# A quarter turn of an 8192 x 8192 matrix: whole loads and two early stores in halves, in place of five loads in three pieces

## The chip, the cores and the metric

The kernel runs on one core of a Trainium2 chip. The metric is the device time of one launch in microseconds. The kernel before took 1281.91 us, the median of three runs that lie between 1279.8 and 1283.59 us. The profiled execution has a span of 1280.1 us from its first to its last instruction, and all times inside a profile are counted from the start of that span.

## The reference

```python
def setup_inputs():
    return {
        "x": np.random.randn(8192, 8192).astype(np.float32),
        "k": 1,
    }

def reference(x: np.ndarray, k: int) -> np.ndarray:
    return np.rot90(x, k)
```

With k = 1 the output element in row i and column j is x[j, 8191 - i]. Nothing is computed; 268.44 MB are read from device memory and 268.44 MB are written back in another order.

## The kernel before

The input is cut into macro tiles of 1024 rows by 4096 columns (eight row tiles of 128 rows each), sixteen of them; the last one is cut again in two halves of four row tiles. A macro tile goes through four steps:

1. **Load.** A row tile of 128 rows x 4096 columns (2 MB, 16 KB in each partition) is loaded into SBUF by a DMA that the SP queue issues. It takes one of two buffers of `a_pool`; in the first macro tile some go to `o_pool`, which stands empty then.
2. **Reverse.** VectorE copies it in eight chunks of 512 columns into buffers of `r_pool` (63 of them, of 2 KB a partition), and turns the order of the columns within each block of 128.
3. **Transpose.** TensorE transposes 128 x 128 blocks into PSUM, 32 for each output.
4. **Store.** ScalarE copies two PSUM tiles of 128 x 2048 into an output tile (16 KB in each partition, three buffers in `o_pool`) and issues the DMA that stores it, from its own queue. A macro tile has eight outputs. Each needs all eight row tiles of its macro tile, one 512-column chunk from each.

The loop that loads. `loads` counts the row tiles, so every 25th is loaded in three pieces, of which the two outer ones have 8 rows:

```python
P = 128
R = 1024
RT = R // P
W = 4096
CH = 512
EVERY = 25
UNEVEN = [(0, 8), (8, P - 8), (P - 8, P)]
F = 4096
FP = 2048
# ... cut ...
    a_pool = ctx.enter_context(tc.tile_pool(name="a_pool", bufs=2))
    r_pool = ctx.enter_context(tc.tile_pool(name="r_pool", bufs=63))
    o_pool = ctx.enter_context(tc.tile_pool(name="o_pool", bufs=3))
    psum_pool = ctx.enter_context(
        tc.tile_pool(name="psum", bufs=2, space=bass.MemoryType.PSUM)
    )
# ... cut ...
        for t in range(rt):
            if loads < RT and loads % 5 >= 2:
                a = o_pool.tile([P, W], dt, tag="o")
            else:
                a = a_pool.tile([P, W], dt, tag="a")
            loads += 1
            for p0, p1 in UNEVEN if loads % EVERY == 0 else [(0, P)]:
                r = r0 + t * P
                nc.sync.dma_start(
                    out=a[p0:p1, :], in_=x[r + p0 : r + p1, c0 : c0 + W]
                )
            for j in range(W // CH):
                ar = r_pool.tile([P, CH // P, P], dt, tag="ar")
                nc.vector.tensor_copy(
                    out=ar[:],
                    in_=a[:, j * CH : (j + 1) * CH].rearrange(
                        "r (b m) -> r b m", m=P
                    )[:, :, ::-1],
                )
                chunks[t, j] = ar
```

The loop that stores. For a macro tile of 1024 rows PW is 2 and G is 4: an output tile holds four groups of 1024 numbers in each partition. S is how many groups go out with one DMA; in the kernel before it is 4 everywhere but in the very last output of the kernel:

```python
        for i, g0 in enumerate(range(0, W // P, G)):
            # ... cut: the output tile ot, from o_pool (every other one from
            # a_pool in the two last, smaller tiles) ...
            o = ot[:, : G * rows].rearrange("m (g f) -> m g f", g=G)
            S = PW if end and r0 + rows == N and g0 + G == W // P else G
            # ... cut: the first output's transposes run tile by tile ...
            for h in range(0, G, PW):
                if h // PW not in ps:
                    psum_tile(h // PW)
                    for w in range(h, h + PW):
                        for t in range(rt):
                            transposes(t, [w])
                nc.scalar.copy(o[:, G - PW - h : G - h, :], ps[h // PW])

                done = h + PW
                if done % S == 0:
                    top = M - c0 - (g0 + done) * P
                    dst = out[top : top + S * P, r0 : r0 + rows].rearrange(
                        "(g m) f -> m g f", g=S
                    )
                    nc.scalar.dma_start(
                        out=dst, in_=o[:, G - done : G - done + S, :]
                    )
```

A pass over the finished program (`whole_reads`) merges the SBUF side of every store into one contiguous read per partition: 16 KB where S is 4, 8 KB where S is 2.

Of the kernel before, what the change touches and what calls it, by code (L numbers as in the profile page):

```python
# [2 lines left out]

# [5 lines left out]
# [8 lines that stand above are left out]
LAST = [4, 4]  # L17
W = 4096
CH = 512
EVERY = 25  # L20
UNEVEN = [(0, 8), (8, P - 8), (P - 8, P)]
F = 4096
FP = 2048


def whole_reads(nc):

    for fn in nc.m.functions:
        for block in fn.blocks:
            for n, ins in enumerate(block.instructions):
                if not isinstance(ins, mybir.InstDMACopy):
                    continue
                src = ins.ins[0]
                ap = [list(d) for d in src.ap]
                if len(ap) == 3 and ap[2][0] == 1 and ap[1][0] == ap[2][1]:  # L40
                    ap = [ap[0], [1, 1], [1, ap[1][1] * ap[2][1]]]
                    block.instructions[n] = copy.replace(
                        ins,
                        ins=[copy.replace(src, ap=ap)],
                        ant_dge_precooked=False,
                    )


def macro_tiles(N, M):

    tiles = [(r0, RT, c0) for r0 in range(0, N, R) for c0 in range(0, M, W)]
    r0, _, c0 = tiles.pop()
    for n in LAST:
        tiles.append((r0, n, c0))
        r0 += n * P
    return tiles


@with_exitstack
def kernel(  # L60
    ctx: ExitStack,
    tc: tile.TileContext,
    x: bass.AP,
    k: bass.AP,
    out: bass.AP,
):
    nc = tc.nc
    assert k == 1, f"only k=1 supported, got {k}"
    nc.at_finalize(whole_reads)

    N, M = x.shape
    dt = x.dtype

    consts = ctx.enter_context(tc.tile_pool(name="consts", bufs=1))
    ident = consts.tile([P, P], dt)
    make_identity(nc, ident)
# [8 lines that stand above are left out]
    loads = 0  # L85

    def load(r0, rt, c0):

        nonlocal loads
        chunks = {}
# [5 lines that stand above are left out]
            else:  # L100
                a = a_pool.tile([P, W], dt, tag="a")
            loads += 1

            for p0, p1 in UNEVEN if loads % EVERY == 0 else [(0, P)]:
                r = r0 + t * P
                nc.sync.dma_start(  # L108
                    out=a[p0:p1, :], in_=x[r + p0 : r + p1, c0 : c0 + W]
                )  # L110
            for j in range(W // CH):
                ar = r_pool.tile([P, CH // P, P], dt, tag="ar")
                nc.vector.tensor_copy(  # L113
# [6 lines that stand above are left out]
            yield chunks  # L120

    def store(r0, rt, c0, chunks, end):

        rows = rt * P
        PW = 1
        while 2 * PW * rows <= FP:  # L130
            PW *= 2
        G = PW
        while 2 * G * rows <= F:
            G *= 2
        for i, g0 in enumerate(range(0, W // P, G)):
            if end and i % 2:
                ot = a_pool.tile([P, F], dt, tag="a")
            else:
                ot = o_pool.tile([P, F], dt, tag="o")
            o = ot[:, : G * rows].rearrange("m (g f) -> m g f", g=G)  # L140

            S = PW if end and r0 + rows == N and g0 + G == W // P else G


            ps = {}

            def transposes(t, ws):
                for w in ws:
                    g = g0 + w
                    nc.tensor.transpose(  # L150
                        ps[w // PW][:, PW - 1 - w % PW, t * P : (t + 1) * P],
                        chunks[t, g * P // CH][:, g % (CH // P), :],
                        ident,
                    )

            def psum_tile(h):
                pt = psum_pool.tile([P, FP], mybir.dt.float32, tag="ps")
                ps[h] = pt[:, : PW * rows].rearrange("m (g f) -> m g f", g=PW)

            if i == 0 and (rt == RT or r0 + rows < N):  # L160
                for h in range(G // PW):
                    psum_tile(h)
                for t in range(rt):
                    transposes(t, range(G))
# [17 lines that stand above are left out]
            yield  # L182

    tiles = macro_tiles(N, M)
    *most, before_last, last = tiles
    for m in most:
        *_, chunks = load(*m)
        for _ in store(*m, chunks, False):
            pass


    *_, chunks = load(*before_last)
    outputs = store(*before_last, chunks, True)
    rows = load(*last)
    for _ in range(last[1] - 1):
        next(rows)
    next(outputs)
    chunks = next(rows)
    for _ in outputs:
        pass  # L200
    for _ in store(*last, chunks, True):
        pass


# [1 line left out]
_INS = ['x', 'k']  # L206
_OUTS = [((8192, 8192), 'float32')]

_NUMBERS = {'k': 1}


# [26 lines left out]
```

## Time and profile before

| what | value |
|---|---|
| device time, median of three | 1281.91 us |
| span of the profiled execution | 1280.1 us |
| bytes moved by DMA, mean rate over the span | 537.55 MB, 420 GB/s |
| row tile loads: whole / in three pieces | 123 / 5 |
| output stores: whole / in two halves | 127 / 1 |
| busy: TensorE, VectorE, ScalarE | 54%, 28%, 37% of the span |
| median time from issue to landing: whole load, whole store | 16.6 us, 25.5 us |

The profile's page cuts the span in 40 slices of 32 us. For each slice it gives the busy tenths of each engine, the mean busy share of the sixteen DMA engines, and the bytes moved in GB/s. A table by windows gives the same for any stretch that is asked for: its length, the busy time of each engine with the number of its instructions, the granted TensorE clock, the busy share of the DMA engines (successive packets overlap by a little in the records, so 1.01 stands for full) and the rate in GB/s. The timeline of an engine lists its instructions in order; in brackets at the end of a line stands how long the engine was idle before it, and what ended that wait.

### The profile page before, as it was taken

The numbers are of one execution on the slowest core, as the hardware profiler recorded it, in microseconds if no ns is written. First come the engines' busy times: TensorE is split into PE (matmuls) and PEld (weight loads), VectorE is DVE, ScalarE is ACT, GpSimd is POOL, SyncE is SP. The second block draws the span as 40 slices with busy tenths as digits, with TensorE's granted clock in tenths as the row PEclk, the third lists the DMA queues.
The fourth block names the chain that finished last, engine by engine and source line by source line (L and its number), as shares of the span: only waits on it lengthen the run. The fifth ranks groups of instructions, "written<-read, shape, count | busy, mean of one in ns | idle before, by whom it ended". The sixth has DMA issues, their size and how long they took to land.

```text
span 1280.1 us, 10428 instructions
## 1 busy us (share of the span) xinstructions
PE 688.8 (54%) x4096; PEld 640.3 (50%) x4096; DVE 355.2 (28%) x1024; ACT 468.1 (37%) x257; POOL 0.7 (0%) x6
## 2 busy tenths in 40 slices
PE   1565556545465555655546545565554645536673
PEld 1455555545464444554536535554454644535673
DVE  4423222232223222223222232223222232223220
ACT  0433334334243432433424424243432443325353
POOL 0000000000000000000000000000000000000000
PEclk9976777868778676776777758677677786777677
DMA  9999999999999999999999999999999999999998
GB/s 401 426 429 429 429 428 398 429 430 428 429 428 429 405 420 429 413 430 428 428 428 399 428 373 428 429 429 428 430 414 429 412 431 427 427 428 418 409 424 341
DMA packets 37137, 537.55 MB, mean 420 GB/s; under 512 B 4192, under 2 KB 4192, under 8 KB 4192
## 3 DMA queue, kind: packets, MB, share of 16 engines
q1 hardware_dynamic: 18512, 268.44, 50.0%
q10 hardware_dynamic: 18576, 268.44, 49.7%
q8 instruction: 32, 0.52, 0.2%
q14 instruction: 17, 0.14, 0.0%
HBM read 268.44 MB, written 268.44 MB: 419 GB/s over the span
## 4 chain that ended last, share of the span: by engine, by line
DMA 81%; DVE 12%; ACT 3%; PE 2%; issue 1%; ACTq 0%; DVEq 0%; SPq 0%
DMA a<-in_x_dram 76%; DVE ar L113 12%; DMA out_dram<-ot 4%; ACT ot L171 3%; PE pt L150 2%; ACTq L179 0%; DVEq L113 0%; SPq L108 0%; ACTq L171 0%
## 5 line engine op out<-in xcount | busy, mean ns | idle before, releaser
L150 PE MATMUL pt<-ident,ar 128*128 128x128 f32 x4096 | 688.8, 345 | 572.2 <-ACT ot L171 377.3
L150 PEld LDWEIGHTS pt<-ident,ar 128*128 128x128 f32 x4096 | 640.3, 183 | 620.5 <-ACT ot L171 414.2
L171 ACT COPY ot<-pt 128x2048 f32<-128x2048 f32 x256 | 466.8, 1870 | 769.6 <-DMA out_dram<-ot 466.3
L113 DVE COPY ar<-a 128x512 f32<-128x512 f32 x1024 | 355.2, 420 | 883.8 <-DMA a<-in_x_dram 757.8
L171 ACT ACT_TABLE_LOAD x1 | 1.3, 1283 | 25.6 <-DVE ar L113 25.6
masks.py:199 POOL TENSOR_SCALAR_AFFINE_SELECT ident<-ident 128x128 f32<-128x128 f32 x1 | 0.3, 292 | 0.1
masks.py:197 POOL MEMSET ident<- 128x128 f32 x1 | 0.2, 205 | 0.3 <-POOLq L219 0.3
L219 POOL MEMSET const-bfloat16-1.0<- 128x1 bf16 x1 | 0.1, 102 | 0.0
L219 POOL MEMSET const-uint8-127<- 128x1 uint8 x1 | 0.1, 102 | 0.0
L219 POOL MEMSET const-float32-0.0<- 128x1 f32 x1 | 0.1, 99 | 0.2 <-issue 0.2
L219 POOL MEMSET const-float32-1.0<- 128x1 f32 x1 | 0.1, 99 | 0.0
## 6 DMA issues: line engine op xcount, KB each, us to landing
out_dram<-ot ACTq DMA_DIRECT2D x127, 2048.0 KB, 25.5
a<-in_x_dram SPq DMA_DIRECT2D x123, 2048.0 KB, 16.6
a<-in_x_dram SPq DMA_DIRECT2D x5, 1792.0 KB, 18.7
out_dram<-ot ACTq DMA_DIRECT2D x2, 1024.0 KB, 15.0
a<-in_x_dram SPq DMA_DIRECT2D x10, 128.0 KB
```

What stands on the lines that cost most here:

```text
L113: nc.vector.tensor_copy(out=ar[:], in_=a[:, j * CH : (j + 1) * CH].rearrange("r (b m) -> r b m", m=P)[:, :, ::-1],)
L150: nc.tensor.transpose(ps[w // PW][:, PW - 1 - w % PW, t * P : (t + 1) * P], chunks[t, g * P // CH][:, g % (CH // P), :], ident,)
L171: nc.scalar.copy(o[:, G - PW - h : G - h, :], ps[h // PW])
L219: nc = _bacc.Bacc("TRN2", target_bir_lowering=False, num_devices=1)
```

## The change: what it does and what it is for

It has two parts. First, the five row tiles whose number is a multiple of 25 are loaded as all others are, with one DMA of 128 rows; the pieces of 8, 112 and 8 rows are gone. Second, the fifth and the seventh output of the first macro tile (i is 4 and 6) are stored in two halves: S is 2 for them, so each half is one DMA of 1 MB whose SBUF reads are 8 KB, and the first half is issued after the first of the two ScalarE copies. While these halves are in the queue beside whole loads, a read of the store queue is half as large as one of the load queue; the second part is there to change how the two queues share the DMA engines for that time. What is computed stays the same.

```diff
-EVERY = 25
-UNEVEN = [(0, 8), (8, P - 8), (P - 8, P)]
 F = 4096
 FP = 2048
# ... cut ...
             loads += 1
-            for p0, p1 in UNEVEN if loads % EVERY == 0 else [(0, P)]:
-                r = r0 + t * P
-                nc.sync.dma_start(
-                    out=a[p0:p1, :], in_=x[r + p0 : r + p1, c0 : c0 + W]
-                )
+            nc.sync.dma_start(
+                out=a[:], in_=x[r0 + t * P : r0 + (t + 1) * P, c0 : c0 + W]
+            )
# ... cut ...
-            S = PW if end and r0 + rows == N and g0 + G == W // P else G
+            lead = r0 == 0 and c0 == 0 and i in (4, 6)
+            S = PW if lead or (end and r0 + rows == N and g0 + G == W // P) else G
```

The order of the instructions on every engine stays as it was, but for the ten DMA issues that fall away on the SP queue and the two that are added on ScalarE's.

## The prediction

> **What bounds the kernel now.** I first read the page. TensorE is busy for 54% of the span, VectorE for 28%, ScalarE for 37%, so none of them is full. The DMA row and the row of rates under it tell the rest:
>
> ```profile
> DMA  9999999999999999999999999999999999999998
> GB/s 401 426 429 429 429 428 398 429 430 428 429 428 429 405 420 429 413 430 428 428 428 399 428 373 428 429 429 428 430 414 429 412 431 427 427 428 418 409 424 341
> ...
> q1 hardware_dynamic: 18512, 268.44, 50.0%
> q10 hardware_dynamic: 18576, 268.44, 49.7%
> ```
>
> The reader is to see that the sixteen DMA engines are taken all the time, and that most slices stand at 428 to 430 GB/s, while some ten fall to between 373 and 420. Nothing is left to win in a slice at 429. What the kernel could lose or gain lies in the dips, and since the engines never have a reserve, a dip is not made up later. Loads (q1) and stores (q10) take half of the engines each.
>
> Second, I asked the chain that ended last where the dips are. It is mostly load after load: a VectorE copy of eight chunks, then about 16.6 us until the next load of that buffer has landed. Five of its loads are longer: 21.0 us from 196.75, 19.7 from 437.27, 20.8 from 697.44, 19.4 from 945.39 and 20.1 from 1185.85. At about 9.8 us a row tile (two loads in each 19.5 us of the chain) these are the places of the row tiles 25, 50, 75, 100 and 125, the ones in three pieces. The chain leaves the loads twice, at 759 and at 914 us, for outputs.
>
> Third, I cut the span around these places with the table by windows (columns: stretch, its us, then the compute engines, the clock, the DMA share and GB/s):
>
> ```profile
> 100.00:190.00 90.00, 51.49 (x284) 48.52 (x284) 24.96 (x72) 32.83 (x18) 0.00 (x0) 0.71 1.01 429
> 190.00:210.00 20.00, 9.98 (x68) 9.07 (x68) 4.93 (x15) 7.74 (x5) 0.00 (x0) 0.75 1.01 379
> ...
> 430.00:465.00 35.00, 20.61 (x132) 19.22 (x132) 8.32 (x24) 14.65 (x8) 0.00 (x0) 0.73 1.01 400
> ...
> 515.00:525.00 10.00, 6.79 (x34) 6.39 (x35) 2.77 (x8) 5.50 (x3) 0.00 (x0) 0.54 0.99 389
> ...
> 670.00:712.00 42.00, 25.39 (x154) 24.00 (x155) 11.09 (x32) 18.29 (x10) 0.00 (x0) 0.70 1.00 405
> ...
> 752.00:769.00 17.00, 8.71 (x50) 8.31 (x51) 5.55 (x16) 6.82 (x4) 0.00 (x0) 0.57 0.86 322
> ...
> 935.00:960.00 25.00, 13.88 (x79) 13.40 (x80) 6.13 (x18) 10.91 (x6) 0.00 (x0) 0.70 1.01 410
> ...
> 1185.00:1212.00 27.00, 18.48 (x93) 17.77 (x91) 5.65 (x17) 8.03 (x5) 0.00 (x0) 0.66 1.01 403
> ```
>
> Two kinds of dip are to be seen. Around the loads in pieces (190, 430, 670, 935, 1185) the engines stay full, a share of 1.00 or 1.01, and yet move less: the same packets take longer. At 515 and 752 the share itself falls, to 0.99 and 0.86; there was not enough to transfer. These lie where a macro tile begins.
>
> Fourth, ScalarE's timeline at the first output of a macro tile, where it waits for TensorE, which waits for the last of eight loads:
>
> ```profile
> 116.95 3.64 ACT L171 COPY ot<-pt 128x2048 f32<-128x2048 f32 x2 [13.08 <-PE pt L150]
> ...
> 277.61 3.64 ACT L171 COPY ot<-pt 128x2048 f32<-128x2048 f32 x2 [15.70 <-PE pt L150]
> ...
> 434.97 3.64 ACT L171 COPY ot<-pt 128x2048 f32<-128x2048 f32 x2 [15.06 <-PE pt L150]
> 517.41 3.64 ACT L171 COPY ot<-pt 128x2048 f32<-128x2048 f32 x2 [18.05 <-PE pt L150]
> ...
> 759.49 3.64 ACT L171 COPY ot<-pt 128x2048 f32<-128x2048 f32 x2 [21.75 <-PE pt L150]
> ...
> 996.34 3.63 ACT L171 COPY ot<-pt 128x2048 f32<-128x2048 f32 x2 [18.25 <-PE pt L150]
> ```
>
> The number in brackets is how long ScalarE had nothing to copy. During it the store queue lives on what was issued before. The wait is 13.1 and 12.3 us at the first two boundaries, 15.7 after row tile 25, 18.0 after 50, 21.8 after 75; after the break at 759 it is 14.7 twice, and 18.3 after 100. So it grows by some 3 us with each load in pieces, and where it reaches 18 us the store queue runs dry: the windows at 515 and 752 are just these two boundaries.
>
> [...]
>
> **The change part by part.**
>
> *Loads in pieces, removed.* Loss of a window = (429 - rate) / 429 x length: 190 to 210 us 2.33, 430 to 465 us 2.37, 670 to 712 us 2.35, 935 to 960 us 1.11, 1185 to 1212 us 1.64; the sum is 9.8 us, all on the path, since the DMA engines are the path. The ten SP issues that fall away, of some 0.33 us each, lie beside other work: 0.
>
> *Boundaries.* In the same way: 515 to 525 us 0.93, 752 to 769 us 4.24, and two more windows of the same answer, 990 to 1010 us at 404 GB/s 1.17 and 1150 to 1170 us at 410 GB/s 0.89; sum 7.2 us. If the wait stays near 13 us, as at the first two boundaries, all of it goes.
>
> *Balance.* [...] In the last 5 us of the span only an engine or two still move data, so one engine's lag sets the end. [...] -3 to +3 us, counted as 0.
>
> *Store halves, added.* Two more issues on ScalarE at 0.55 us, beside its wait of 6.1 us before each copy: 0. [...] the loads get 4.9 us more for each, if buffers let them: some 10 us for both. No bytes are added, so this saves nothing by itself; it moves loads ahead of stores, and the wait at the boundaries from 13 to perhaps 3 to 8 us, so that none runs dry.
>
> *Sum.* 1281.9 - 9.8 - 7.2 = 1264.9, rounded to 1265.
>
> **The rivals.** (1) *The pieces were what kept the sixteen engines together.* Then without them the lag grows, boundaries run dry in spite of the halves, and the time is 1272 if only the direct loss goes, or above 1282 if more is lost. For it: a lag at the end is there. Against it: the boundary wait hardly moves where no piece falls (13.1 to 12.3, 14.7 to 14.7) and jumps where one does. (2) *The halves do nothing or harm:* the reads of 8 KB count as half as fast, or the loads that run ahead stand before VectorE, which waits for a free chunk of the 63, and give the gain back. Then the time is that of removal alone, 1265 to 1270. For it: VectorE already waits for TensorE at times, 126 us in all. (3) *The ends are all that counts:* the slow windows are hidden. That would leave 1281, but full engines with no reserve speak against it.
>
> **Range and chances.** The 9.8 us I hold for nearly sure; of the 7.2 some may come back elsewhere, and the end may go either way by 3. That gives 1260 to 1272. Faster by over 2% means below 1256.3, more than everything counted here and the best case at the end together; 3%. Slower by over 2% needs rival 1 in full: 2%.
>
> **What would show it.** In the profile after: q1 with 18,432 packets and q10 with 18,864; no slice below some 420 GB/s but the first and last; no load of 19 to 21 us in the chain; ScalarE's wait at the boundaries below 13 us throughout, falling right after the first macro tile. A wait that grows without the pieces, or a share below 1 at a boundary, would prove rival 1. A first boundary still at 13 us would prove rival 2 in its first form.

## The result and the profile after

The changed kernel takes 1267.49 us, the median of six runs between 1266.92 and 1267.88; the kernel before takes 1282.1 us in the same comparison. The ratio is 0.9888 with a 95% interval of 0.9876 to 0.9901: 14.6 us are gone. The profiled execution has a span of 1265.4 us in place of 1280.1.

From the page of the changed kernel, the rates in 40 slices and the two DMA queues (q10 stores, q1 loads):

```profile
GB/s 398 428 428 430 427 428 429 429 431 428 428 429 427 430 429 430 428 430 429 428 428 430 429 430 428 428 430 428 429 430 428 429 427 430 426 428 427 428 380 355
...
q10 hardware_dynamic: 18864, 268.44, 50.0%
q1 hardware_dynamic: 18432, 268.44, 49.7%
```

Every slice between the first and the last two stands at 426 to 431 GB/s; the dips to 373 to 420 are gone. One new dip has come, 380 GB/s, just before the end. The packets are as many as the prediction named: 18,432 for 128 loads and 18,864 for 131 stores, 144 for each DMA whether it moves 2 MB or 1 MB. In the kernel before a load in three pieces took 160, (18,512 - 123 x 144) / 5.

The table by windows, at six of the places where the kernel before fell to 322 to 410 GB/s (stretch, its us, compute engines, clock, DMA share, GB/s), and the new dip from a second table of the same kernel:

```profile
190.00:210.00 20.00, 13.37 (x68) 12.89 (x68) 5.55 (x16) 7.27 (x4) 0.00 (x0) 0.66 1.00 428
430.00:465.00 35.00, 22.58 (x120) 21.87 (x121) 8.32 (x24) 13.14 (x8) 0.00 (x0) 0.67 1.01 429
515.00:525.00 10.00, 5.94 (x32) 5.70 (x32) 2.77 (x8) 3.63 (x2) 0.00 (x0) 0.66 1.02 433
670.00:712.00 42.00, 26.16 (x144) 25.03 (x142) 11.26 (x33) 14.54 (x8) 0.00 (x0) 0.71 1.00 428
752.00:769.00 17.00, 9.74 (x53) 9.51 (x54) 5.39 (x16) 7.27 (x4) 0.00 (x0) 0.71 1.01 429
935.00:960.00 25.00, 15.65 (x82) 14.94 (x80) 7.89 (x23) 8.20 (x5) 0.00 (x0) 0.69 1.01 429
```

```profile
1205.00:1232.00 27.00, 20.32 (x139) 19.10 (x140) 4.01 (x12) 17.64 (x10) 0.00 (x0) 0.81 0.89 373
```

ScalarE's timeline at the first output of the third and the twelfth macro tile:

```profile
191.92 3.63 ACT L167 COPY ot<-pt 128x2048 f32<-128x2048 f32 x2 [6.13 <-PE pt L146]
...
900.27 3.64 ACT L167 COPY ot<-pt 128x2048 f32<-128x2048 f32 x2 [6.13 <-PE pt L146]
```

The wait of 12 to 22 us for the last load of a macro tile has vanished. After the first macro tile these are the only two boundaries where a wait of more than 4 us is put down to TensorE, and 6.1 us is what ScalarE waits before any copy, for an output buffer to be stored. The chain of waits has changed with it: it ran through loads for 76% of the span before, now it runs through stores for 81%.

In what follows the loss of a window is, as in the prediction, (429 - rate) / 429 times its length.

### The profile page after: what moved, and what is told of

Read it like the earlier page. It is cut to its first block, busy times and chain, and to the rows that moved or that the text cites. A ratio compares the mean times of both kernels' runs of the same rounds, so it can differ in the third digit from the quotient of the medians.

```text
span 1265.4 us, 10391 instructions
## 1 busy us (share of the span) xinstructions
PE 721.2 (57%) x4096; PEld 680.0 (54%) x4096; DVE 355.2 (28%) x1024; ACT 466.6 (37%) x257; POOL 0.7 (0%) x6
## 3 DMA queue, kind: packets, MB, share of 16 engines
q10 hardware_dynamic: 18864, 268.44, 50.0%
q1 hardware_dynamic: 18432, 268.44, 49.7%
## 4 chain that ended last, share of the span: by engine, by line
DMA 84%; ACT 13%; issue 1%; PE 0%; ACTq 0%; DVE 0%; SPq 0%
DMA out_dram<-ot 81%; ACT ot L167 13%; DMA a<-in_x_dram 3%; PE pt L146 0%; ACTq L175 0%; DVE ar L106 0%; ACTq L167 0%; SPq L101 0%
## 5 line engine op out<-in xcount | busy, mean ns | idle before, releaser
L146 PE MATMUL pt<-ident,ar 128*128 128x128 f32 x4096 | 721.2, 357 | 526.2 <-ACT ot L167 470.2
L146 PEld LDWEIGHTS pt<-ident,ar 128*128 128x128 f32 x4096 | 680.0, 191 | 567.2 <-ACT ot L167 505.0
```

Of the source, the lines that this page charges most:

```text
L146: nc.tensor.transpose(ps[w // PW][:, PW - 1 - w % PW, t * P : (t + 1) * P], chunks[t, g * P // CH][:, g % (CH // P), :], ident,)
```

## The experiments

### Each part by itself

Whole loads, no halved stores:

```diff
-            lead = r0 == 0 and c0 == 0 and i in (4, 6)
-            S = PW if lead or (end and r0 + rows == N and g0 + G == W // P) else G
+            S = PW if end and r0 + rows == N and g0 + G == W // P else G
```

> The loads are whole, no store is halved. Theory A (the pieces cost 9.8 us in their own windows and, through a growing wait at the boundaries, 7.2 us more; the halves only move loads ahead and cost some 3 us at the end, where the store queue of the changed kernel ran dry at 1210 to 1228 us): the wait of ScalarE at the first boundary is 13 us again and stays between 12 and 17 us, no window at a boundary falls below 420 GB/s but perhaps a late one, the gap near the end is gone or smaller, and the time is 1264 to 1267 us. Rival B (the halves are what keeps the boundaries full): the wait grows beyond 18 us without them, boundaries run dry as before, and the time is 1270 to 1275 us.

It takes 1268.03 us (four runs, 1267.17 to 1268.48; ratio to the kernel before 0.9893, 0.9878 to 0.9908). Of the 14.6 us the whole loads bring 13.9. ScalarE's wait at two of its boundaries:

```profile
116.79 3.64 ACT L166 COPY ot<-pt 128x2048 f32<-128x2048 f32 x2 [13.13 <-PE pt L145]
...
983.48 3.63 ACT L166 COPY ot<-pt 128x2048 f32<-128x2048 f32 x2 [14.45 <-PE pt L145]
```

It is between 12.2 and 14.7 us at all fourteen, where the kernel before went from 12 to 22: without the pieces the wait hardly grows (12.7 us at 904, 14.5 at 983), as theory A says. But five late boundaries still dip, where theory A allowed for a late one: 746 to 764 us at 414 GB/s, 905 to 921 at 416, 980 to 1001 at 406, 1063 to 1080 at 408, 1143 to 1158 at 423; 3.3 us in all. The engines are not idle in these windows, their share is 1.00 to 1.01. From 985 to 994 us, in the deepest of them, the queues have (packets, MB, share of the engines' time)

```profile
q1 hardware_dynamic: 153, 2.21, 68.4%
q10 hardware_dynamic: 83, 1.16, 30.4%
```

The stores have less to move, and the loads have 68.4% of the time; but they move 2.21 MB in it, where 68.4% of 429 GB/s over 9 us would be 2.64. The stores move what their share gives, 1.16 MB where 30.4% would be 1.17. Why load rows are slow there was not tested. In return there is no gap near the end: from the windows of this kernel,

```profile
980.00:1001.00 21.00, 13.45 (x89) 12.53 (x90) 5.55 (x16) 10.92 (x6) 0.00 (x0) 0.74 1.00 406
...
1205.00:1232.00 27.00, 20.61 (x154) 19.17 (x153) 5.55 (x16) 15.66 (x10) 0.00 (x0) 0.89 1.00 423
```

The same 27 us stand at 373 GB/s in the changed kernel, a loss of 3.5 us. So the two halves took away 3.3 us at the boundaries and cost about as much at the end.

The five loads in pieces, the two outputs halved:

```diff
-            S = PW if end and r0 + rows == N and g0 + G == W // P else G
+            lead = r0 == 0 and c0 == 0 and i in (4, 6)
+            S = PW if lead or (end and r0 + rows == N and g0 + G == W // P) else G
```

> The five loads stay in pieces, the two outputs are halved. Theory A: the dips around the pieces stay at about 2 us each (9.8 us in all), but the boundaries no longer run dry in the first half of the run, since the wait starts some 10 us lower and grows by 3 us for each load in pieces. The time is 1281.9 - 7.2 + 3 for the gap at the end, some 1275 to 1279 us. Rival B (the halves make the gain): 1268 to 1271 us. Rival C (the halves do nothing without whole loads): 1281 to 1283 us.

It takes 1282.17 us (ratio 1.0002, 0.9992 to 1.0013): nothing is gained, as rival C has it, though not for its reason. The halves do work: the wait at the third boundary is 9.5 us in place of 15.7. But each load in pieces then adds 3.4 to 4.6 us (9.0 to 13.6, 12.3 to 16.9, 16.0 to 19.3), and the later boundaries dip all the same. Windows at three of these boundaries and at one load in pieces:

```profile
747.00:771.00 24.00, 14.78 (x100) 13.62 (x100) 5.55 (x16) 11.01 (x6) 0.00 (x0) 0.72 0.95 380
...
909.00:930.00 21.00, 15.22 (x100) 14.06 (x100) 5.55 (x16) 11.01 (x6) 0.00 (x0) 0.72 0.99 396
933.00:961.00 28.00, 17.71 (x86) 17.24 (x87) 7.72 (x23) 10.91 (x6) 0.00 (x0) 0.65 1.01 405
990.00:1014.00 24.00, 14.40 (x100) 13.16 (x100) 5.55 (x16) 11.01 (x6) 0.00 (x0) 0.73 0.94 371
```

With 832 to 850 us (402 GB/s) and 1154 to 1171 (404) the boundaries lose 9.7 us, more than the 7.2 that the prediction counts for the kernel before; the five windows around the pieces lose 6.7.

One half only, the fifth output, with whole loads:

```diff
-            lead = r0 == 0 and c0 == 0 and i in (4, 6)
+            lead = r0 == 0 and c0 == 0 and i == 4
```

> Whole loads, and only the fifth output is halved: half the lead. Theory A: the first boundary waits some 8 us, no boundary runs dry, and the gap near the end shrinks from 3 us to 0 to 1.5 us; 1264 to 1266 us, the fastest of all. Rival (the gap near the end does not come from the lead): 1267 us as the changed kernel.

It takes 1267.0 us (1266.73 to 1267.79; ratio 0.9887, 0.9872 to 0.9901), the same as the changed kernel. The expectation missed twice: no boundary waits 8 us for TensorE, and the gap stays (1202 to 1228 us at 380 GB/s, 3.0 us). The second half adds no lead that lasts. In the first 150 us loads and stores move 42.24 and 21.04 MB with one half, 42.22 and 20.99 with two, 41.45 and 21.81 with none. The second half does push the loads ahead at first, 5.29 MB against 3.33 from 110 to 130 us of the changed kernel. Then VectorE waits for a free chunk, which TensorE still has to read:

```profile
135.38 2.77 DVE L106 COPY ar<-a 128x512 f32<-128x512 f32 x8 [6.82 <-PE pt L146]
```

The next load waits up to 10.1 us for VectorE, and from 130 to 140 us the lead of the second half is given back:

```profile
q10 hardware_dynamic: 212, 3.06, 72.4%
q1 hardware_dynamic: 92, 1.25, 29.1%
```

### What is slow about a load in pieces

The first three runs keep the two halved outputs and change how the row tiles 25, 50, 75, 100 and 125 are cut. First 112 and 16 rows:

```diff
-UNEVEN = [(0, 8), (8, P - 8), (P - 8, P)]
+UNEVEN = [(0, P - 16), (P - 16, P)]
```

> As the kernel with pieces and halves, but the pieces are of 112 and 16 rows[...]. Theory A1 [...]: dips of 1.5 to 2.5 us around each of the five loads stay, and the time is as with 8, 112 and 8 rows, 1275 to 1279 us. Rival A2 [...]: the dips are gone, 1267 to 1269 us.

It takes 1274.0 us (ratio 0.9939, 0.9922 to 0.9955), between what A1 and A2 forecast. The windows come from the slowest of its four runs, 1277.15 us; the others take 1273.38 to 1274.58. The dips stay: 1.40, 1.12, 1.64, 1.19 and 1.54 us, 6.9 together, as much as the 6.7 of 8, 112 and 8 rows. The third of them:

```profile
678.00:705.00 27.00, 16.43 (x96) 15.67 (x95) 6.96 (x21) 8.85 (x5) 0.00 (x0) 0.75 1.00 403
```

A2 forecast no dips, and falls as to these. How the rows of a piece are shared out among the engines no view shows. In all, the kernel is 8 us faster than with 8, 112 and 8 rows. Its wait starts lower and stays lower (13.5 us at the last boundaries in place of 16.8 to 19.3), and the worst of its boundaries, 980 to 1010 us at 399 GB/s, loses 2.1 us.

Then two pieces of 64 rows:

```diff
-UNEVEN = [(0, 8), (8, P - 8), (P - 8, P)]
+UNEVEN = [(0, 64), (64, P)]
```

> As the kernel with pieces and halves, but the five loads are cut into two pieces of 64 rows[...]. Theory A1 ([...] being cut in two costs nothing): no dip above 0.5 us at the five places, the wait at the boundaries does not grow by more than 1 us at each, 1267 to 1269 us. Rival A3 (any cut of a load costs[...]): dips of 1 to 1.5 us each and a growing wait stay, 1272 to 1275 us as with 112 and 16 rows.

It takes 1277.91 us (ratio 0.9981, 0.9972 to 0.999). Theory A1, by which two pieces of 64 rows should cost nothing, falls: they cost more than 8, 112 and 8 rows, not less. Rival A3 has the direction, but less than the size. The window around the second of these loads, and the next, undisturbed one:

```profile
430.00:456.00 26.00, 13.46 (x79) 12.99 (x80) 6.79 (x20) 10.56 (x6) 0.00 (x0) 0.80 1.01 397
456.00:678.00 222.00, 124.34 (x724) 117.02 (x721) 61.90 (x179) 80.65 (x45) 0.00 (x0) 0.78 1.01 429
```

The five lose 2.33, 1.94, 2.18, 1.82 and 2.18 us, 10.4 together. The stores beside them, which are whole, are slow too: from 430 to 456 us they have 50.2% of the engines' time and move 5.19 MB, or 200 GB/s, while in the 222 us after it 50.6% of the time gives 215 GB/s.

Last, the same five loads in two halves by columns, with one store halved near each so that neither queue gains on the other:

```diff
+TRAIL = [25, 50, 75, 100, 125]
+BOTH = [16, 41, 66, 91, 116]
 # ... cut ...
+            for w in [0, W // 2] if loads in TRAIL else [None]:
+                c, n = (0, W) if w is None else (w, W // 2)
+                nc.sync.dma_start(
+                    out=a[:, c : c + n],
+                    in_=x[r0 + t * P : r0 + (t + 1) * P, c0 + c : c0 + c + n],
+                )
 # ... cut ...
-            lead = r0 == 0 and c0 == 0 and i in (4, 6)
+            stores += 1
+            lead = (r0 == 0 and c0 == 0 and i in (4, 6)) or stores in BOTH
```

> The changed kernel, with the same five loads cut into two halves by columns instead of by rows (all 128 partitions, 8 KB packets), and one output beside each of them halved too, so that neither queue gains on the other. As many DMAs, pieces and bytes as with two pieces of 64 rows[...]. Theory A4 [...]: no dip above 0.5 us at the five places, 1267 to 1269 us. Rival A3 (the cut itself costs): dips of 2 us each, 1276 to 1279 us as with two pieces of 64 rows.

It takes 1267.82 us (1267.66 to 1267.98; ratio 0.9888, 0.9872 to 0.9905). The windows around the second and the third of the loads:

```profile
425.00:450.00 25.00, 17.06 (x107) 16.07 (x106) 8.04 (x24) 10.91 (x6) 0.00 (x0) 0.78 1.01 426
...
670.00:695.00 25.00, 16.51 (x102) 15.76 (x101) 6.98 (x20) 10.91 (x6) 0.00 (x0) 0.77 1.00 426
```

At all five places the loss is 0.1 to 0.2 us, where A4 forecast at most 0.5 and A3 2. That is not the doing of the halved stores beside them: the run below that cuts the load of row tile 118 alone, with no halved store near it, stands at 427 and 428 GB/s from 1090 to 1115 and to 1133 us, while that load is moved. So two DMAs with packets of half the size, each on all 128 partitions, cost 0.1 to 0.2 us here. What costs is a cut by rows, 1.1 to 2.3 us for a load of 2 MB, with the engines full all the while, at a share of 1.00 to 1.01. Why, no run shows. The runs show that it is the cut by rows and not the cut as such; since each row goes to a partition of its own, they don't tell the partitions that a piece writes from the rows of memory that it reads.

Ten DMAs of 8 rows on memory only: the changed kernel with copies to a spare tensor, meant to give some engines more to do than others. In the loop two of them stand at every 25th load, but nothing holds them back, and the trace has all ten issued between 52 and 210 us.

```diff
+            if loads % 25 == 0:
+                for p in range(2):
+                    k0 = (2 * (loads // 25 - 1) + p) * 8
+                    nc.sync.dma_start(
+                        out=spare[k0 : k0 + 8, :],
+                        in_=x[r0 + t * P + 8 * p : r0 + t * P + 8 * p + 8, c0 : c0 + W],
+                    )
```

> The changed kernel, with ten more DMAs of 8 rows each that copy from the input to a spare tensor in device memory, early in the run (the output stays the same; 1.3 MB more are read and written). [...] no SBUF partition is touched by it. Theory A1 (uneven work by itself is not what hurts): 1267.5 plus at most 3 us, since only the end shows it, and no boundary runs dry. Rival A2 (uneven work makes the wait at the boundaries grow and runs them dry): a wait that is 5 us longer than in the changed kernel from the third boundary on, dips there, 1273 to 1280 us.

It takes 1277.75 us, in nine runs from 1274.58 to 1284.89 (ratio 0.9982, 0.9965 to 1.0). The wait rises from 9.0 us at 198.57 to 15.4 at 281.64, as rival A2 has it, and the boundary at 590 to 616 us loses 2.2 us. But the run doesn't separate what it was made for: the spare rows stand in the queue of the loads, and hold them back whether unevenness matters or not, so the 6.4 us by which the wait rises can't be put down to it. That some engines had more to do was the author's assumption, which no view shows. What uneven work does to the wait stays open.

### The gap near the end

The changed kernel, with the load of row tile 118 cut in two column halves, the mirror of a halved store; then 117 and 118.

```diff
+TRAIL = [118]
 # ... cut ...
+            for w in [0, W // 2] if loads in TRAIL else [None]:
```

> The changed kernel, with the load of row tile 118 cut into two column halves, so that its packets are 8 KB while the stores beside it have 16 KB: the mirror of the halved stores, shortly before the end. Theory A (the gap of 3.1 us near the end is there because the loads end too far ahead of the stores, and the three output buffers then hold too little to store): the stores catch up by some 5 us, the gap shrinks to 0 to 1.5 us, 1264.5 to 1266.5 us. Rival (the gap has another cause, the order of the last outputs): 1267.5 us, gap as before.

> The same with row tiles 117 and 118: the stores catch up by some 10 us. Theory A: the gap is gone, ScalarE waits for TensorE some 8 to 14 us at the last boundary, 1264 to 1265.5 us. Rival: 1267.5 us.

They take 1267.99 us (ratio 0.9901, 0.9887 to 0.9916) and 1268.85 us (0.9909, 0.9894 to 0.9924), so nothing was won. ScalarE's wait at the last whole macro tile, first with one load cut, then with two, each from its own timeline:

```profile
1140.26 3.63 ACT L171 COPY ot<-pt 128x2048 f32<-128x2048 f32 x2 [14.18 <-PE pt L150]
```

```profile
1145.76 3.63 ACT L171 COPY ot<-pt 128x2048 f32<-128x2048 f32 x2 [23.23 <-PE pt L150]
```

One cut moves a queue by 23.2 - 14.2 = 9.0 us against the other. The windows with one load cut:

```profile
1133.00:1157.00 24.00, 13.76 (x93) 12.85 (x94) 5.55 (x16) 11.01 (x6) 0.00 (x0) 0.72 0.97 392
1205.00:1232.00 27.00, 22.14 (x154) 20.99 (x152) 5.55 (x16) 15.82 (x10) 0.00 (x0) 0.80 1.01 426
```

The gap is gone, 426 GB/s in place of 373, so it did come from loads that end too far ahead of the stores. But the boundary before it now loses 2.1 us, and with two loads cut 6.4 us (1125 to 1163 us at 357 GB/s). The rest is in the last stretch of the run:

| kernel | boundaries, us | 1205 to 1232, us | after that, to the end of the span, us | sum, us | span, us |
|---|---|---|---|---|---|
| whole loads only | 3.3 | 0.4 | 6.7 | 10.4 | 1266.7 |
| one store halved | 0 | 3.2 | 6.5 | 9.7 | 1266.0 |
| changed kernel | 0 | 3.5 | 5.5 | 9.0 | 1265.4 |
| one load cut | 2.1 | 0.2 | 7.2 | 9.5 | 1265.7 |
| two loads cut | 6.4 | 0.3 | 3.4 | 10.1 | 1266.4 |

The span less the sum is 1256.2 to 1256.4 us in every row, so these three columns hold the whole difference between the kernels. What is taken from one column comes back nearly in full in another. From 1260 us on the DMA engines of the changed kernel are only 0.2 busy or less, as if a few of the sixteen ended late. The author's reading is that a pause in which the others wait lets these catch up, and that a slowest engine sets this floor. It fits all the rows, but it was argued from them: no view shows the engines one by one, and no run gave the late ones less to do.

## Why the prediction was right, and where it wasn't

The time lies within the range, 2.5 us above the sum of 1265.

*Loads in pieces, removed: 9.8 us.* Right in kind and nearly in size. After the change the first four windows stand at 428 and 429 GB/s; the fifth, at 422, runs into the gap near the end. Some 0.9 of the 9.8 us belongs to the boundaries: 670 to 684 us stands at 401 GB/s, and that load in pieces is issued at 686.6 us. The five are issued at 186.9, 436.6, 686.6, 935.6 and 1185.1 us, so three of the long loads of the chain (196.75, 697.44, 945.39) are the loads behind the ones in pieces. Why a load in pieces is slow was not shown. It isn't that some of its pieces are small: two of 64 rows cost more, 2.1 us a load against 1.3 for 8, 112 and 8 rows with the same halved stores.

*Boundaries: 7.2 us, all of it to go if the wait stays near 13 us.* The size came out, since the changed kernel loses nothing at its boundaries, but the condition was wrong. With whole loads alone the wait stays at 12 to 15 us, as said, and 3.3 us are lost all the same; it takes the halved stores to save them. "Where it reaches 18 us the store queue runs dry", as the prediction put it, was read from one kernel and doesn't hold: whole loads alone lose 0.5 us at a wait of 12.7, the halves with pieces 2.7 us at 16.9, while the kernel before lost nothing at 17.3 (590 to 612 us at 429 GB/s). The length of the wait is one part of it; late in the run less of it is enough. That the engines have then drifted apart would explain it; this is a guess, which no run tested.

*Balance: counted as 0, -3 to +3.* The range was the author's estimate; no view shows how the pieces load the single engines. What the trace has is the rate, 34 GB/s from 1275 us to the end of the kernel before, 1.3 times a sixteenth of 429. The count held: the last 28.1 us of the kernel before lose 6.4 us (331 GB/s), the last 33.4 us of the changed one 5.5 (358 GB/s), so 0.9 us was gained.

*Store halves: 0, and 10 us of lead for both, so that the wait goes from 13 to 3 to 8 us.* This is the term that was mis-sized: the time it adds is not 0 but 3.5 us, the gap near the end. Loads do gain beside the halves: from 70 to 104 us of the changed kernel the queues moved

```profile
q1 hardware_dynamic: 548, 7.93, 54.5%
q10 hardware_dynamic: 599, 6.65, 46.1%
```

so 7.93 MB against 6.65. From 110 to 120 us, where nearly all stores are halves, it is 2.85 against 1.46 MB in nearly equal numbers of packets, 200 and 195. The 4.9 us for each halved output are an estimate, which these counts and the 429 GB/s bear out: if packets go in equal numbers, 2.10 MB of stores in reads of 8 KB go beside 4.19 MB of loads, 14.7 us in all, where whole reads have 2.10 beside 2.10 in 9.8 us. But what the loads gain by it the stores lose too, and the wait is the distance between the two: twice 4.9 by this estimate, measured as 9.0 for one cut load more. The second half, in turn, gave its gain back at 130 to 140 us. What lasted was 1.6 MB of lead (42.22 - 20.99 against 41.45 - 21.81), some 7 us at half of 429 GB/s. So the wait of at most 6.1 us lies in the prediction's 3 to 8, but by two errors that work against each other, which is luck. The lead that lasted came back as the gap. The sum put right is 9.8 + 7.2 + 0.9 - 3.5 = 14.4 us, against 14.6 measured.

*The rivals.* Rival 2 was closer than it was given credit for: the time is that of removal alone, 1267.5 against 1268.0, within the spread of the runs. Its second form, loads that run ahead and give the gain back, is what happened: the second half gave its lead back before VectorE, and the lead of the first cost 3.5 us at the end. Rival 1 is out as to the time, since removing the pieces alone gives 1268.0; what there is to it are the 3.3 us that late boundaries then still lose. Rival 3 is out, since the slow windows were gained back nearly in full.

*Signs.* The packet counts, and waits below 13 us right after the first macro tile, came as named. "No slice below 420 but the first and last" failed in one slice, the 380. That the chain has no load of 19 to 21 us says little, since it now runs through stores and has two loads in all.

## What to carry to other kernels

When the DMA engines are full, cut a transfer by columns and not by rows: with all 128 partitions in each piece a cut of a 2 MB load cost 0.1 to 0.2 us here, with fewer 1.1 to 2.3 us. Read the rate beside the busy share: at a share of 1.01 the engines stood at 397 GB/s in one window and at 429 in the next. A load that comes late can cost twice if a later stage needs a whole group of loads (whole loads brought 13.9 us here, where the windows around the five lost 9.8): look at the wait at the start of each group, and whether it grows from one to the next. A DMA cut into packets of half the size beside whole ones in the other queue moved the two queues against each other, by 9.0 us for one load here. One halved output was enough, a second was given back as soon as the buffers were full, and the lead that lasted was paid for where the run ended.

## What the runs showed that was not expected

Two pieces of 64 rows cost 2.1 us for a 2 MB load, more than the 1.3 us of 8, 112 and 8 rows, while two column halves cost 0.1 to 0.2. And five kernels with dips in quite different places, 0 to 6.4 us at the boundaries and 0.2 to 3.5 us near the end, all ended between 1267.0 and 1268.9 us.
